# Changing how a one-core decoder-layer kernel starts: the order of its first loads, transposes and products

## Chip, core and metric

The kernel runs on one core of one Trainium2 chip. The metric is the device time in microseconds (us) of one execution; several executions of the same program are timed, and the median is compared. PE is TensorE's matmul side, PEld its weight loads, DVE VectorE, ACT ScalarE, POOL GpSimd and SP SyncE, which issues most of the DMAs here.

## What is computed

One layer of a decoder trunk, 512 tokens by 1024 features, in float32:

```python
h = x
xn = rmsnorm(h, g_attn)
proj = xn @ w_in                                   # 1024 x 3072
sb_q, sb_k, sb_v, d_q, d_k, d_v = split(proj)      # 6 x 512 columns
mix = concat(stick_breaking(sb_q, sb_k, sb_v),     # 8 heads of 64
             rmsnorm(differential(d_q, d_k, d_v, lam, rel_bias), g_subln) * 0.2)   # lambda_init 0.8, so 1 - 0.8
h = h + mix @ w_o
u = causal_depthwise_conv(rmsnorm(h, g_ffn) @ w_up, conv_w, conv_b)   # 1024 x 5632
gate, val = split(u)
h = h + (gelu(gate) * val) @ w_down
h = h + sigmoid(rmsnorm(h, g_ple) @ w_ple_gate) * (p @ w_ple_proj)
out = rmsnorm(h, g_final)
```

The stick-breaking weights are `A[t,s] = beta_ts * prod_{s<j<t}(1 - beta_tj)` with `beta = sigmoid(q k / 8)`. `lam` is `exp(lambda_q1 . lambda_k1) - exp(lambda_q2 . lambda_k2) + 0.8`, and `rel_bias` is a table that is looked up by the distance of query and key.

## The kernel before

Every float32 product is made of three matmuls (`mm3`, lines 121 to 123) on operands that are split into a rounded high part and the rest: high times high, high times low, low times high. Weights come with 1 MB or 512 KB loads on SP's queue into two buffers `wraw`; `split_w` (lines 140, 141) makes `whi` on ACT and `wlo` on DVE of 128 columns (or two row blocks) at a time, three pairs of buffers. All of x is kept transposed: eight tiles of 128 features by 512 tokens, each scaled by `g_attn` and split into `xgh` (ACT, line 330) and `xgl` (DVE, line 331).

PE runs in the order in which the code is written, by hand; the other engines' order is made by a scheduler that knows the dependences and priorities. Weight pieces stand in a list, in the order q and k of heads' pair 0, q and k of pair 1, v, and so on; `units(n)` runs the next n steps of that list, and for q, k and v one step is one feature tile, three matmuls of 512 columns. The attention's own steps (`pair_steps` for the four pairs of stick-breaking heads, `diff_steps` for the four differential heads) alternate with units by a written plan.

The start, in `stages`: x comes in four chunks of 256 features (`load_x`, line 310), 512 KB each. SP issues chunk 0, the q weights of pair 0, chunk 1, the k weights of pair 0, chunks 2 and 3, then further weights. PE runs `warm` (line 740): products of `identR` with itself, 128 columns, results unused. Then the transpose of the `g_attn` row (line 196), the eight transposes of chunk 0 (line 324), eight products more, the transposes of chunk 1, four products more, four units of piece 0 (tiles 0 to 3), the transposes of chunks 2 and 3, and the rest of pieces 0 and 1. `keep_x` copies the transposes unscaled to memory, `norm_x` makes `rstd1`, the norm of each token (POOL, line 148).

After two more units `bcast_rstd1` spreads `rstd1` over the partitions: DVE casts it (`bch`, line 154), PE runs eight small products (line 158), DVE copies the result (`rb`). Only then the q and k of pair 0, which stay in PSUM until here (`late`), can be scaled and split (lines 387 to 389). Six units later PE makes the first logits (lines 492 and 500), with two buffers `z`; ACT makes two sigmoids of each (`cum` line 524, `beta` line 525), DVE a running product (line 531). The third logits of a pair reuse the first `z`, so they wait for the second sigmoid on it.

The parameters of later stages (`params`) are loaded on ACT's queue at a place of the plan between pairs 1 and 2: gains, biases and convolution weights (lines 208 to 213), the lambdas (line 229), a table of distances (line 250). What does not depend on PE there may be put earlier by the scheduler: the two sums for `lam` on DVE (line 233) and their exp on ACT (`lexp`, line 238) run ahead of the first sigmoid.

Of the kernel before, what the change touches and what calls it, by code (L numbers as in the profile page):

```python
# [11 lines left out]
F32 = mybir.dt.float32  # L12
F32R = mybir.dt.float32r
# [5 lines left out]
P = 128  # L19
T = 512  # L20
D = 1024
KT = D // P
NB = T // P
HD = 64
# [6 lines left out]
NBUCK = 32  # L31
NMAP = 8
EPS = 1e-6
NEG = -1e30
# [4 lines left out]
YW = T + P  # L39


class Kern:
# [42 lines left out]
    def rest(self):  # L85
        for _ in self.flow:
            pass
# [36 lines left out]

    def load_w(self, src, kts, cols, raw=None):

        if raw is None:
            raw = self.wraw.tile([P, kts, cols], F32, tag="wraw", name=self.nm("wraw"))
        for off, ap in src:
            n = ap.shape[1]  # L130
            self.nc.sync.dma_start(raw[:, :, off : off + n], ap.rearrange("(k p) n -> p k n", p=P))
        return raw
# [31 lines left out]
    def consts(self):  # L164
        nc, a = self.nc, self.a
        c = self.cpool = self.open("consts")
# [31 lines left out]

    def params(self, pst):
        nc, a, c = self.nc, self.a, self.cpool  # L200

# [10 lines left out]
        self.gcol["w0"], n1 = r, r + 2 * FT  # L212
        nc.scalar.dma_start(rows2[0 : 4 * FT, :], a["conv_w"][0, 1:3].rearrange("t (r p) -> (t r) p", p=P))
        self.par = c.tile([P, n1], F32, name="par1")
        self.par2 = c.tile([P, 4 * FT], F32, name="par2")
        ps = pst()
# [6 lines left out]
        nc.vector.tensor_scalar(self.gsub, self.g("sub", 0), 1.0 - LAMBDA_INIT, None, op0=ALU.mult)  # L223


        rest = next(spare)
        lt = rest[:, : 4 * HD].rearrange("p (a d) -> p a d", a=4)
        for i, key in enumerate(("lambda_q1", "lambda_k1", "lambda_q2", "lambda_k2")):
            nc.scalar.dma_start(lt[:, i, :], a[key].partition_broadcast(P).rearrange("p o d -> p (o d)"))
        s = c.tile([P, 2], F32, name="lsum")  # L230
        junk = rest[:, 4 * HD : 5 * HD]
        for i in range(2):
            nc.vector.tensor_tensor_reduce(
                out=junk, in0=lt[:, 2 * i, :], in1=lt[:, 2 * i + 1, :], scale=1.0, scalar=0.0,
                op0=ALU.mult, op1=ALU.add, accum_out=s[:, i : i + 1],
            )
# [4 lines left out]
        nc.vector.scalar_tensor_tensor(self.neglam, e[:, 1:2], -LAMBDA_INIT, e[:, 0:1], op0=ALU.add, op1=ALU.subtract)  # L241


        tab = c.tile([NBUCK + 1, NMAP], F32, name="tab")
        nc.gpsimd.memset(tab, NEG)
        nc.scalar.dma_start(tab[0:NBUCK, :], a["rel_bias"])
        sk = self.dram.tile([NMAP, YW], F32, name="sk")
        for lo, n in ((0, T), (T, P)):
            oh, y = next(spare)[: NBUCK + 1, :n], next(spare)[:NMAP, :n]
            nc.scalar.dma_start(oh, a["onehot"][:, lo : lo + n])  # L250
# [6 lines left out]
        nc.scalar.dma_start(self.sk2, bass.AP(sk.tensor, sk.offset, [[YW, NMAP], [0, P], [1, YW]]))  # L257

# [76 lines left out]

    def behind_x(self, do):

        with self.tc.issue_after(self.last[0]), self.tc.issue_after(self.last[1]):
            do()
# [202 lines left out]
    def split_t(self, ps, n, c=""):  # L542
        nc = self.nc
        hi, lo = (x[:, :n] for x in self.parts("tw", c))
        nc.scalar.copy(hi, ps[:, :n])  # L545
        nc.vector.tensor_sub(lo, ps[:, :n], hi.bitcast(F32))  # L546
        return hi, lo
# [165 lines left out]
    def stages(self):  # L713
# [19 lines left out]
        self.xn = self.su.tile([P, NB, D], F32, name="xn")  # L733
        self.load_x((0,))
# [10 lines left out]
        def first_load():  # L745
            cols = self.qk_cols(self.qoff[0], self.koff[0])
            raw = self.load_w(cols[:1], KT, 2 * P)
            self.load_x((1,))
            self.load_w(cols[1:], KT, 2 * P, raw)
            self.load_x((2, 3))  # L750
            return raw

        self.add_qk(0)
        self.raws[0] = first_load
        self.add_qk(1)
# [7 lines left out]
        self.add_wo(4, True, lambda nt, ps: self.residual(nt, ps, "ffn", self.h1g, self.sqacc))  # L763
        self.load_raws(0)
# [5 lines left out]
        def begin(i):  # L770
            self.behind_x(lambda: self.prepare(i))
            if i < 2:
                first.append(self.pieces[i][2](*self.splits[i]))
# [12 lines left out]
        px += next(steps)  # L786
        begin(2)
        self.behind_x(self.norm_x)
        for k in range(2, KT):
            self.keep_x(k, px[k])  # L790
        todo(1, 4)
        todo(0, 5)
        todo(1, 5)
        self.flow = self._flow(2)
# [17 lines left out]

        self.units(2)
        self.bcast_rstd1(psh)
# [18 lines left out]


# [218 lines left out]
```

## Time and profile before

| | |
|---|---|
| time, median of 3 runs | 706.27 us (704.77 to 706.96) |
| the profiled execution | 706.06 us, span 704.3 us |
| PE busy | 685.5 us, 97% of the span |
| DVE, ACT, POOL busy | 441.1, 313.8, 42.5 us |
| granted TensorE clock, mean | 0.993 |

The span is the time from the first to the last instruction of the profiled execution; its own time is 1.8 us longer. A matmul's row gives a start and a modelled end; matmuls overlap, so the distance from start to start tells how fast PE goes. A 512-column product takes 0.23 us at 2.4 GHz and 0.43 to 0.44 us at 1.2 GHz. The granted clock's record begins at the first event, so its column reads 1.00 in the first 14 us too, where the starts are 0.44 us apart.

### The profile page before, as it was taken

The page shows a single profiled execution, that of the slowest core. Times are in us where ns is not written, and L with a number is a line of the kernel's source. Part 1 is how long each engine was busy: PE and PEld are TensorE (multiplying, and loading weights), DVE is VectorE, ACT ScalarE, POOL GpSimd, SP SyncE. Part 2 cuts the span into 40 slices and gives each one's busy share as a digit, 9 for nine tenths or more (in the row PEclk, how much of TensorE's full clock was granted, in tenths as well). Part 3 has the DMA queues.
Part 4 walks back from the last instruction along what each step waited for, and adds up shares of the span by engine and source line. Part 5 has one row for each costly group of instructions (what it writes and reads, how often), then busy time and mean ns, then how long its engine had stood idle before and what let it go on. Part 6 is the DMA issues. An engine that isn't in the chain of part 4 may idle for free. (4 is left out here: it accounts for less than half of the span.)

```text
span 704.3 us, 8244 instructions
## 1 busy us (share of the span) xinstructions
PE 685.5 (97%) x3263; PEld 562.3 (80%) x3263; DVE 441.1 (63%) x663; ACT 313.8 (45%) x471; POOL 42.5 (6%) x52
## 2 busy tenths in 40 slices
PE   8879999999999999999999999999999999999995
PEld 8668877787888887888888888888888888888885
DVE  3775769668666858498777777677734232436445
ACT  4654435556553543365444444444423232326422
POOL 2200000000100024100000000000000020202001
PEclk9989999999999999999999999999999999999999
DMA  9522135232326111223322233321323133127002
GB/s 288 200 69 60 60 108 192 60 94 76 106 85 209 61 60 60 90 90 121 119 77 86 78 120 119 97 84 60 123 101 105 61 104 120 45 92 239 29 27 93
DMA packets 66809, 71.64 MB, mean 102 GB/s; under 512 B 2360, under 2 KB 55850, under 8 KB 66771
## 3 DMA queue, kind: packets, MB, share of 16 engines
q1 hardware_dynamic: 63376, 64.76, 28.8%
q10 hardware_dynamic: 2755, 4.27, 1.8%
q0 software_dynamic: 640, 2.10, 0.8%
q8 instruction: 25, 0.41, 0.3%
q14 instruction: 13, 0.11, 0.0%
HBM read 66.90 MB, written 6.84 MB: 105 GB/s over the span
## 5 line engine op out<-in xcount | busy, mean ns | idle before, releaser
L140 ACT CAST whi<-wraw 128x1024 fp32r<-128x1024 f32 (+1 forms) x102 | 105.5, 1034 | 151.0 <-PE mm L122 128.3
L141 DVE TENSOR_TENSOR wlo<-wraw,whi 128x1024 fp32r<-128x1024 f32 (+1 forms) x102 | 123.5, 1211 | 74.4 <-ACT whi L140 73.4
L121 PE MATMUL mm<-xgh,whi 128*128 128x512 f32 x128 | 53.9, 421 | 0.2 <-DVE v_sb L511 0.2
L122 PE MATMUL mm<-xgl,whi 128*128 128x512 f32 x128 | 51.6, 403 | 0.0
L123 PE MATMUL mm<-xgh,wlo 128*128 128x512 f32 x128 | 51.4, 401 | 0.0
L878 DVE TENSOR_TENSOR vpad<-mm,rb 128x512 f32<-128x512 f32 x44 | 30.1, 688 | 33.8 <-PE mm L123 33.7
L699 POOL TENSOR_TENSOR sqacc<-sqacc,sq 128x512 f32<-128x512 f32 x14 | 23.1, 1653 | 359.6 <-issue 254.9
L880 ACT ACTIVATE y<-vpad,par,par 128x512 f32<-128x512 f32 x44 | 35.5, 814 | 2.7 <-DVE vpad L878 2.5
L882 DVE SCALAR_TENSOR_TENSOR y<-vpad,par,y 128x512 f32<-128x512 f32 x44 | 33.1, 751 | 1.3
L881 DVE SCALAR_TENSOR_TENSOR y<-vpad,par,y 128x512 f32<-128x512 f32 x44 | 32.8, 746 | 0.0
L121 PEld LDWEIGHTS mm<-xgh,whi 128*128 128x128 f32 x128 | 25.2, 197 | 6.8 <-issue 1.1
L884 ACT ACTIVATE y<-y 128x512 f32<-128x512 f32 x22 | 13.9, 631 | 34.9 <-DVE y L882 34.9
L123 PEld LDWEIGHTS mm<-xgh,wlo 128*128 128x128 f32 x128 | 24.9, 194 | 5.6
L122 PEld LDWEIGHTS mm<-xgl,whi 128*128 128x128 f32 x128 | 25.1, 196 | 4.6 <-DVE xgl L331 0.3
L531 DVE TENSOR_TENSOR_SCAN cum<-cum,fresh 128x512 f32<-128x512 f32 x20 | 23.6, 1212 | 4.2 <-ACT cum L524 4.2
L492 PE MATMUL z<-k,q 64*128 64x512 f32 (+3 forms) x192 | 20.6, 340 | 5.2 <-ACT beta L525 3.7
L121 PE MATMUL mm<-whi,xgh 128*128 128x512 f32 x64 | 25.5, 398 | 0.0
L122 PE MATMUL mm<-wlo,xgh 128*128 128x512 f32 x64 | 25.0, 390 | 0.0
L123 PE MATMUL mm<-whi,xgl 128*128 128x512 f32 x64 | 25.0, 390 | 0.0
L492 PEld LDWEIGHTS z<-k,q 64*128 64x128 f32 x192 | 15.5, 189 | 10.9 <-ACT beta L525 4.2
L636 ACT ACTIVATE pr<-pr,nmx 128x512 f32<-128x512 f32 (+3 forms) x32 | 17.6, 552 | 12.2 <-DVE nmx L632 12.0
L546 DVE TENSOR_TENSOR twl<-z,twh 128x1024 fp32r<-128x1024 f32 (+2 forms) x20 | 18.4, 954 | 7.1 <-ACT twh L545 7.0
(538 smaller groups left out, 1759.4 us busy)
## 6 DMA issues: line engine op xcount, KB each, us to landing
wraw<-in_w_up SPq DMA_DIRECT2D x22, 1024.0 KB, 5.0
wraw<-in_w_in SPq DMA_DIRECT2D x16, 512.0 KB, 5.2
wraw<-in_w_down SPq DMA_DIRECT2D x8, 1024.0 KB, 5.0
wraw<-in_w_in SPq DMA_DIRECT2D x4, 1024.0 KB, 6.1
wraw<-in_w_o SPq DMA_DIRECT2D x4, 1024.0 KB
wraw<-in_w_ple_gate SPq DMA_DIRECT2D x4, 1024.0 KB, 8.2
wraw<-in_w_down SPq DMA_DIRECT2D x4, 768.0 KB, 4.3
sk<-sk ACTq DMA_DIRECT2D x1, 2560.0 KB
```

The source lines that it names most:

```text
L121: nc.tensor.matmul(ps, lhsT=l[0], rhs=r[0], start=start, stop=False, **kw)
L122: nc.tensor.matmul(ps, lhsT=l[0], rhs=r[1], start=False, stop=False, **kw)
L123: nc.tensor.matmul(ps, lhsT=l[1], rhs=r[0], start=False, stop=stop, **kw)
L140: nc.scalar.copy(hi, raw)
L141: nc.vector.tensor_sub(lo, raw, hi.bitcast(F32))
L492: nc.tensor.matmul(z[:, h, col : col + n], lhsT=q[o, x, tb * P : (tb + 1) * P], rhs=k[o, y, :n], start=i == 0 and at == 0, stop=i == 2 and ...
L531: nc.vector.tensor_tensor_scan(back, back, fresh, 1.0, op0=ALU.mult, op1=ALU.max)
L699: nc.gpsimd.tensor_add(sqacc, sqacc, sq)
L878: nc.vector.tensor_mul(u[:, 2 : T + 2], ps, rb2)
L880: nc.scalar.activation(y, u[:, 2 : T + 2], AF.Identity, scale=self.cw(2, ch), bias=self.g("cb", ch))
L881: nc.vector.scalar_tensor_tensor(y, u[:, 1 : T + 1], self.cw(1, ch), y, op0=ALU.mult, op1=ALU.add)
L882: nc.vector.scalar_tensor_tensor(y, u[:, 0:T], self.cw(0, ch), y, op0=ALU.mult, op1=ALU.add)
```

## The change

The zeros: a 128x512 tile `nought` is set to zero on DVE and cast; `warm(n)` now multiplies it by itself, 512 columns a product. Nine stand first, one between the transposes of chunks 0 and 1.

The loads: the q weights of pair 0 come in two halves by rows (features 0 to 511 and 512 to 1023), the first one ahead of all x, then chunks 0 and 1, the second half, chunks 2 and 3, and only then the two halves of the k weights. Each half is cast and split by itself.

The products: after the transposes of chunk 1 two units of piece 0, the transposes of chunk 2, two units, the transposes of chunk 3, the other four units, then piece 1 (the k weights) as a whole. `split_t` now records its last instructions, and `behind_x` is called `behind`.

The broadcast: `units(5)` instead of `units(2)` stand ahead of `bcast_rstd1`; the last entry of the plan of the pairs has 8 units instead of 11.

The parameters: `params` becomes a generator. Its loads are issued from entry 4 of the plan on, the rest runs at entry 8 behind the last split. The sums and the exp for `lam` become `lambdas`, behind the last split of pair 3.

```diff
@@ consts
+        nought = su.tile([P, T], F32, name="nought")
+        nc.vector.memset(nought, 0.0)
+        self.nought = su.tile([P, T], F32R, name="noughtR")
+        nc.vector.tensor_copy(self.nought, nought)
@@ params
+        rest = next(spare)
+        lt = rest[:, : 4 * HD].rearrange("p (a d) -> p a d", a=4)
+        for i, key in enumerate(("lambda_q1", "lambda_k1", "lambda_q2", "lambda_k2")):
+            nc.scalar.dma_start(lt[:, i, :], a[key].partition_broadcast(P).rearrange("p o d -> p (o d)"))
...
+        for lo, n in ((0, T), (T, P)):
+            hot[lo] = next(spare)[: NBUCK + 1, :n]
+            nc.scalar.dma_start(hot[lo], a["onehot"][:, lo : lo + n])
+        yield
...
+    def lambdas(self):
+        nc, c = self.nc, self.cpool
+        s = c.tile([P, 2], F32, name="lsum")
+        for i in range(2):
+            nc.vector.tensor_tensor_reduce(
...
+        nc.scalar.activation(e, s, AF.Exp)
@@ stages
-                nc.tensor.matmul(busy[:, :P], lhsT=self.identR, rhs=self.identR, start=True, stop=True)
-
-        warm(12)
+                nc.tensor.matmul(busy, lhsT=self.nought[:, :P], rhs=self.nought, start=True, stop=True)
+
+        warm(9)
...
+        load(0, 0)
+        self.load_x((0, 1))
+        load(0, 1)
+        self.load_x((2, 3))
+        load(1, 0)
+        load(1, 1)
...
-        px = next(steps)
-        begin(0)
-        for k in range(2):
-            self.keep_x(k, px[k])
-        warm(8)
-        px += next(steps)
-        begin(1)
-        warm(4)
-        todo(0, 4)
+        split(0, 0)
+        px = next(steps)
+        warm(1)
+        px += next(steps)
+
+        self.behind(lambda: split(0, 1))
+        self.behind(lambda: [self.keep_x(k, px[k]) for k in range(2)])
+        todo(0, 2)
         px += next(steps)
+        todo(0, 2)
         px += next(steps)
-        begin(2)
-        self.behind_x(self.norm_x)
...
+        self.behind(lambda: [split(1, h) for h in range(2)])
         todo(0, 5)
-        todo(1, 5)
...
+        self.behind(rest)
+        todo(1, 9)
@@
-        self.units(2)
+        self.units(5)
         self.bcast_rstd1(psh)
@@
-            plan += [(p, 0, 3), (p, 1, 12), (p, 2, 4), (p, 3, 4), (p, 4, 4 if p == 2 else 11)]
+            plan += [(p, 0, 3), (p, 1, 12), (p, 2, 4), (p, 3, 4), (p, 4, 4 if p == 2 else 8)]
@@
+            if i == 4:
+                params = self.params(self.psm)
+                next(params)
             if i == 8:
-                self.params(self.psm)
+                self.behind(lambda: next(params, None))
@@
+        self.behind(self.lambdas)
```

On PE at the very start, before (`z_101` and `z_102` take the transposes of chunks 0 and 1, `mm_195` is piece 0):

```order
L740 MATMUL mm_103<-identR 128x128 x12
L196 MATMUL z_102<-ident,rows_116 128x8
L324 MATMUL z_101<-ident,xn 128x128 x8
L740 MATMUL mm_103<-identR 128x128 x8
L324 MATMUL z_102<-ident,xn 128x128 x8
L740 MATMUL mm_103<-identR 128x128 x4
L121 MATMUL mm_195<-xgh_142,whi_150 128x512
L122 MATMUL mm_195<-xgl_143,whi_150 128x512
L123 MATMUL mm_195<-xgh_142,wlo_151 128x512
```

The same place after (`mm_187` is piece 0, `mm_194` takes transposes of chunk 2):

```order
L751 MATMUL mm_106<-noughtR 128x512 x9
L200 MATMUL z_105<-ident,rows_116 128x8
L335 MATMUL z_104<-ident,xn 128x128 x8
L751 MATMUL mm_106<-noughtR 128x512
L335 MATMUL z_105<-ident,xn 128x128 x8
L121 MATMUL mm_187<-xgh_154,whi_133 128x512
L122 MATMUL mm_187<-xgl_155,whi_133 128x512
L123 MATMUL mm_187<-xgh_154,wlo_134 128x512
L121 MATMUL mm_187<-xgh_158,whi_133 128x512
L122 MATMUL mm_187<-xgl_159,whi_133 128x512
L123 MATMUL mm_187<-xgh_158,wlo_134 128x512
L335 MATMUL mm_194<-ident,xn 128x128 x4
```

The small products are gone from between the transposes, and the transposes of chunk 2 stand after two feature tiles of piece 0 instead of four.

On ACT ahead of the first sigmoid, before (`q_381` and `k_386` belong to pair 0, `mix4l` and the like are tiles that hold parameters):

```order
L388 CAST q_381<-qkt_382 128x512
L229 DMA mix4l_845<-in_lambda_q 128x64
L229 DMA mix4l_845<-in_lambda_k 128x64
L388 CAST k_386<-qkt_387 128x512
L229 DMA mix4l_845<-in_lambda_q 128x64
L229 DMA mix4l_845<-in_lambda_k 128x64
L250 DMA mix5h_846<-in_onehot 33x512
L250 DMA mix6h_848<-in_onehot 33x128
L238 ACTIVATE lexp<-lsum 128x2
L140 CAST whi_450<-wraw_247 128x1024
L388 CAST q_409<-qkt_410 128x512
L524 ACT_TABLE_LOAD
```

The same place after (the q cast of pair 0 stands just ahead; two lambdas and the one-hot tables follow behind the first two sigmoids):

```order
L140 CAST whi_410<-wraw_255 128x1024
L399 CAST k_391<-qkt_392 128x512
L213 DMA mix4h_659<-in_g_ffn 8x128
L213 DMA mix4h_659<-in_g_ple 8x128
L213 DMA mix4h_659<-in_g_subln 1x128
L399 CAST q_405<-qkt_406 128x512
L213 DMA mix4h_659<-in_conv_b 44x128
L216 DMA mix4h_659<-in_conv_w 44x128
L218 DMA mix4h_659<-in_conv_w 88x128
L222 DMA mix4l_660<-in_lambda_q 128x64
L222 DMA mix4l_660<-in_lambda_k 128x64
L535 ACT_TABLE_LOAD
```

`lexp` is gone from here, the loads of gains and convolution weights have come here from ahead of the q cast, and a weight cast stands ahead of the k cast.

On DVE ahead of the first differential head, before (`k_1402` is that head's k, `av_1355` and `v_diff` are work of pair 3 and of v):

```order
L595 TENSOR_TENSOR av_1355<-z_1356,av_1355 64x512
L832 TENSOR_TENSOR v_diff<-vd,v_diff 128x2x512 x2
L595 TENSOR_TENSOR av_1355<-z_1356,av_1355 64x512
L387 SCALAR_TENSOR_TENSOR qkt_1403<-mm_1351,rb_366 128x512
L141 TENSOR_TENSOR wlo_1408<-wraw_1279,whi_1407 128x1024
L598 TENSOR_TENSOR mix3l_1378<-av_1355,mix3h_1377 128x512
L389 TENSOR_TENSOR k_1402<-qkt_1403,k_1402 128x512
```

The same place after:

```order
L268 SCALAR_TENSOR_TENSOR neglam<-lexp 128x1
L607 TENSOR_TENSOR av_1353<-z_1354,av_1353 64x512
L862 TENSOR_TENSOR v_diff<-vd,v_diff 128x2x512 x2
L398 SCALAR_TENSOR_TENSOR qkt_1392<-mm_1340,rb_371 128x512
L607 TENSOR_TENSOR av_1353<-z_1354,av_1353 64x512
L141 TENSOR_TENSOR wlo_1397<-wraw_1268,whi_1396 128x1024
L400 TENSOR_TENSOR k_1391<-qkt_1392,k_1391 128x512
```

The last of `lambdas` stands ahead, k's scaling has moved ahead of the second `av`, and the split of pair 3's result behind k.

## Rows read from the trace of the kernel before

**Rows 1.** Windows: stretch, busy PE, PEld, DVE, ACT, POOL (count), granted clock, DMA share, GB/s

```profile
42.00:44.00 2.00, 0.55 (x4) 0.55 (x6) 1.48 (x2) 2.00 (x3) 0.00 (x0) 0.54 0.92 273
...
49.00:50.00 1.00, 1.00 (x6) 0.83 (x5) 1.00 (x2) 0.00 (x0) 0.00 (x0) 1.00 0.00 0
```

**Rows 2.** Timeline of PE's start: start, us, engine, line, operation, out<-in, count [idle before <-releaser]

```profile
1.91 2.82 PE L740 MATMUL mm<-identR 128*128 128x128 f32 x12 [1.91 <-DVE identR L181]
...
4.87 1.97 PE L324 MATMUL z<-ident,xn 128*128 128x128 f32 x8
...
8.64 1.94 PE L324 MATMUL z<-ident,xn 128*128 128x128 f32 x8 [0.20 <-DMA xn<-in_x]
...
11.12 0.73 PE L121 MATMUL mm<-xgh,whi 128*128 128x512 f32 x1
...
14.64 0.51 PE L123 MATMUL mm<-xgh,wlo 128*128 128x512 f32 x1
...
15.70 1.04 PE L324 MATMUL mm<-ident,xn 128*128 128x128 f32 x8
```

**Rows 3.** Timeline of ACT and DVE at the start, one split of a tile of x

```profile
8.38 0.69 ACT L330 ACTIVATE xgh<-z,gattn 128x512 fp32r<-128x512 f32 x1 [0.82 <-DVE xgl L331]
...
9.10 0.75 DVE L331 SCALAR_TENSOR_TENSOR xgl<-z,gattn,xgh 128x512 fp32r<-128x512 f32 x1 [0.76 <-ACT xgh L330]
```

**Rows 4.** Timeline of PE around the broadcast, the third logits, and pair 1's third logits

```profile
26.72 0.39 PE L122 MATMUL mm<-xgl,whi 128*128 128x512 f32 x1
26.95 0.39 PE L123 MATMUL mm<-xgh,wlo 128*128 128x512 f32 x1
29.45 0.33 PE L158 MATMUL z<-identR,bch 128*128 128x128 f32 x1 [2.12 <-DVE bch L154]
...
43.45 1.01 PE L492 MATMUL z<-k,q 64*128 64x256 f32 x6 [3.75 <-ACT beta L525]
...
44.87 0.73 PE L121 MATMUL mm<-xgh,whi 128*128 128x512 f32 x1
...
48.82 0.48 PE L121 MATMUL mm<-xgh,whi 128*128 128x512 f32 x1
...
69.68 0.62 PE L492 MATMUL z<-k,q 64*128 64x256 f32 x6
...
70.51 0.45 PE L121 MATMUL mm<-whi,xgh 128*128 128x512 f32 x1
```

**Rows 5.** Timelines of ACT (its queue's issues as ACTq), then of DVE, 27 to 42 us

```profile
27.02 1.04 ACT L140 CAST whi<-wraw 128x1024 fp32r<-128x1024 f32 x1
...
28.46 0.46 ACTq L211 DMA_DIRECT2D mix4h<-in_conv_w  x1
...
32.13 0.62 ACT L388 CAST q<-qkt 128x512 fp32r<-128x512 f32 x1 [4.07 <-DVE qkt L387]
...
38.49 0.20 ACT L238 ACTIVATE lexp<-lsum 128x2 f32<-128x2 f32 x1 [4.51 <-DVE lsum L233]
...
40.16 1.28 ACT L524 ACT_TABLE_LOAD   x1
41.46 1.02 ACT L524 ACTIVATE cum<-z 128x1024 f32<-128x1024 f32 x1
...
28.10 1.23 DVE L141 TENSOR_TENSOR wlo<-wraw,whi 128x1024 fp32r<-128x1024 f32 x1 [0.41 <-ACT whi L140]
29.24 0.16 DVE L154 CAST bch<-rstd 128x4 fp32r<-128x4 f32 x1
```

**Rows 6.** DMA issues: out<-in, engine, operation, count, KB each, median us to landing

```profile
wraw<-in_w_in SPq DMA_DIRECT2D x4, 1024.0 KB, 6.1
```

**Rows 7.** Waits of SP's queue: who waited for whom, us in total, times, longest

```profile
SPq L131 <- DMA mix4h<-in_conv_w: 5.3, 1, 5.3
```

**Rows 8.** Timeline of PE at the first differential head's logits

```profile
164.53 1.77 PE L492 MATMUL z<-k,q 64*128 64x512 f32 x18 [0.76 <-DVE k L389]
```

More of the change, by code (lines that the diff above doesn't have):

```diff
@@ L123, in mm3, with load_w @@
         nc.tensor.matmul(ps, lhsT=l[1], rhs=r[0], start=False, stop=stop, **kw)
-    def load_w(self, src, kts, cols, raw=None):
+    def load_w(self, src, kts, cols, raw=None, r0=0):
         if raw is None:
@@ L223, in params @@
         nc.vector.tensor_scalar(self.gsub, self.g("sub", 0), 1.0 - LAMBDA_INIT, None, op0=ALU.mult)
[L226 to L236, printed above, removed]
-        e = c.tile([P, 2], F32, name="lexp")
-        nc.scalar.activation(e, s, AF.Exp)
-        self.neglam = c.tile([P, 1], F32, name="neglam")
[L241 to L246, printed above, removed]
+        self.lt, self.junk = lt, rest[:, 4 * HD : 5 * HD]
         sk = self.dram.tile([NMAP, YW], F32, name="sk")
         for lo, n in ((0, T), (T, P)):
-            oh, y = next(spare)[: NBUCK + 1, :n], next(spare)[:NMAP, :n]
-            nc.scalar.dma_start(oh, a["onehot"][:, lo : lo + n])
+            oh, y = hot[lo], next(spare)[:NMAP, :n]
             ps = pst()
@@ L257, in params @@
         nc.scalar.dma_start(self.sk2, bass.AP(sk.tensor, sk.offset, [[YW, NMAP], [0, P], [1, YW]]))
+    def lambdas(self):
[3 more added lines that the diff above has]
+            nc.vector.tensor_tensor_reduce(
+                out=self.junk, in0=self.lt[:, 2 * i, :], in1=self.lt[:, 2 * i + 1, :], scale=1.0, scalar=0.0,
+                op0=ALU.mult, op1=ALU.add, accum_out=s[:, i : i + 1],
+            )
+        e = c.tile([P, 2], F32, name="lexp")
+        nc.scalar.activation(e, s, AF.Exp)
+        self.neglam = c.tile([P, 1], F32, name="neglam")
+        nc.vector.scalar_tensor_tensor(self.neglam, e[:, 1:2], -LAMBDA_INIT, e[:, 0:1], op0=ALU.add, op1=ALU.subtract)
     def mix_tile(self, i, x):
@@ L334, in prep_x, with behind @@
             yield banks
-    def behind_x(self, do):
+    def behind(self, do):
         with self.tc.issue_after(self.last[0]), self.tc.issue_after(self.last[1]):
@@ L544, in split_t @@
         hi, lo = (x[:, :n] for x in self.parts("tw", c))
-        nc.scalar.copy(hi, ps[:, :n])
-        nc.vector.tensor_sub(lo, ps[:, :n], hi.bitcast(F32))
+        a = nc.scalar.copy(hi, ps[:, :n])
+        b = nc.vector.tensor_sub(lo, ps[:, :n], hi.bitcast(F32))
+        self.last = (a.ins, b.ins)
         return hi, lo
@@ L739, in warm, with load @@
             for _ in range(n):
-                nc.tensor.matmul(busy[:, :P], lhsT=self.identR, rhs=self.identR, start=True, stop=True)
-        warm(12)
+                nc.tensor.matmul(busy, lhsT=self.nought[:, :P], rhs=self.nought, start=True, stop=True)
+        warm(9)
         self.params_attn(lambda: zs[1][:, 0, :])
[L745 to L751, printed above, removed]
+        half = KT // 2
+        cols = self.qk_cols(self.qoff[0], self.koff[0])
+        raw = self.wraw.tile([P, KT, 2 * P], F32, tag="wraw", name=self.nm("wraw"))
+        def load(j, h):
+            self.load_w(cols[j : j + 1], half, 2 * P, raw[:, h * half : (h + 1) * half, :], h * half * P)
+        load(0, 0)
[4 more added lines that the diff above has]
+        load(1, 1)
         self.add_qk(0)
-        self.raws[0] = first_load
+        self.raws[0], self.nraw = raw, 1
         self.add_qk(1)
@@ L768, in stages, with split, rest @@
         first = []
[L770 to L773, printed above, removed]
+        for i in range(2):
+            self.splits.append([self.wsp.tile([P, KT, P], F32R, tag=t, name=self.nm(t)) for t in ("whi", "wlo")])
+            first.append(self.pieces[i][2](*self.splits[i]))
+        def split(i, h):
+            r, k = raw[:, :, i * P : (i + 1) * P], slice(h * half, (h + 1) * half)
+            hi, lo = (x[:, k, :] for x in self.splits[i])
+            a = nc.scalar.copy(hi, r[:, k, :])
+            b = nc.vector.tensor_sub(lo, r[:, k, :], hi.bitcast(F32))
+            self.last = (a.ins, b.ins)
         todo = lambda i, n: [next(first[i], None) for _ in range(n)]
+        split(0, 0)
         px = next(steps)
-        begin(0)
-        for k in range(2):
-            self.keep_x(k, px[k])
-        warm(8)
+        warm(1)
         px += next(steps)
-        begin(1)
-        warm(4)
-        todo(0, 4)
+        self.behind(lambda: split(0, 1))
+        self.behind(lambda: [self.keep_x(k, px[k]) for k in range(2)])
+        todo(0, 2)
         px += next(steps)
+        todo(0, 2)
         px += next(steps)
-        begin(2)
-        self.behind_x(self.norm_x)
-        for k in range(2, KT):
-            self.keep_x(k, px[k])
-        todo(1, 4)
-        todo(0, 5)
-        todo(1, 5)
+        self.behind(lambda: [split(1, h) for h in range(2)])
+        todo(0, 5)
+        def rest():
+            self.prepare(2)
+            self.norm_x()
+            for k in range(2, KT):
+                self.keep_x(k, px[k])
+        self.behind(rest)
+        todo(1, 9)
         self.flow = self._flow(2)
```

9 lines of the change are left out of this document (6 added, 3 removed).

## The prediction

> **What bounds the kernel now.** First the page: PE is busy nearly the whole span, so only its waits and its clock can give time. Then the waits of PE alone: the two longest lie in the first 50 us, where the change works. There I read the timelines of PE, ACT and DVE side by side. They show four losses. The products that count start at 11.12, and the ninth starts at 14.64, so they are 0.44 us apart, against 0.23 us later (26.72 to 26.95): PE runs at 1.2 GHz, not 2.4, until then, although it had been busy with 128-column products and transposes from 1.91 on [rows 2, 4]. PE idles 2.12 us at 29.45 for the broadcast of rstd [rows 4]. It idles 3.75 us at 43.45, because ACT starts the first sigmoid only at 41.46: `lexp` had held ACT 4.51 us for the lambdas' loads, and a table load of 1.28 us came on top [rows 4, 5]. And during that idle time the granted clock falls to half (0.54 from 42 to 44, 1.00 again from 49) [rows 1].
>
> I call the 24 products of one 128-column weight piece a piece, and three products a unit. The sum is made against the profiled execution, 706.06 us (span 704.3 and 1.8 around it); the median of the runs is 706.27.
>
> **The change, part by part.**
> *Zero products.* Twelve plus twelve 128-column products become nine of 512 columns, and one more later. At 0.44 us each and from about 1.9 (the memset and cast of zeros on DVE take the place of the wait for `identR`, [rows 2]) nine end at 5.9. Before, PE reached the first transposes at 4.87, so this alone costs about 1 us. It pays only if the clock is full afterwards. The trace of before does not show a product on zeros, so the value lies between no effect and full clock from about 6. I take full clock: both times that PE ran 512-column products without a break from half clock, it had it after eight or nine of them, 11.12 to 14.64 and 44.87 to 48.82 [rows 2, 4].
>
> *Loads.* The last x chunk has 2.5 MB ahead of and with it, not 3; the second 1.25, not 1.5. PE waited for the second until 8.64 [rows 2]; five sixths of that is 7.2, I take 7.5. The last was there by 15.70 with 3 MB, so by 13.1 with 2.5. The halved weights cost one issue more on SP and land early; ACT has cast the first half before x is there, so nothing on the path.
>
> *Alternation.* With the clock full: transposes of chunk 0 (1.04 us for eight [rows 2]) 5.9 to 6.9, of chunk 1 7.5 to 8.5. ACT and DVE then split four tiles in turn at 0.69 and 0.75 [rows 3]: 8.0 + 2 x 0.69 + about 0.8 puts the second tile's low half at 10.2. Six products end at 10.65, chunk 2 at 11.65, six more (6 x 0.227) at 13.0, chunk 3 at 14.0. Then 42 products are left of the 54 that stand ahead of the broadcast before: 14.0 + 9.55 + 0.25 for the last tile's split = 23.8, where before had 15.70, sixteen transposes and the same 42 and was done at 27.2.
>
> *Broadcast nine products later* (units 5, not 2, ahead of it). PE gets there at 23.8 + 9 x 0.227 = 25.85. DVE's order still puts a weight split ahead of the broadcast's cast, as before (28.10, then 29.24 [rows 5]). That split needs a 1 MB load into the buffer of the first weights, free when DVE has split their last half: chunk 3's tiles until 16.45, two half splits 17.7. Load 6.1 [rows 6], cast 1.04, split 1.23, then 0.4: the broadcast is at **26.5**, a wait of 0.65. If that load landed earlier, the wait is nothing; if it took 2 us more, 2.65. Gain here: 29.45 - 26.5, plus nine products already done, 2.05: **5.0**.
>
> *Parameters' work later.* `lexp`, the two reductions and their wait leave ACT and DVE. From the broadcast, the q cast comes 2.68 later (32.13 [rows 5]) and lasts 0.62; then the order has a weight cast (1.04) and the k cast (0.62): 5.0 after the broadcast. Then eight issues of parameters' loads on ACT, which before stood mostly ahead of the broadcast: 0.3 to 0.46 each (one is 0.46 [rows 5]), 3 to 3.5, the third q cast runs beside them; the table load 1.28, two sigmoids of 1.02 less 0.1 overlap, and 0.3 for the steps between: 11.9 after the broadcast the first z is free. PE has the broadcast, 18 products and two logits to do, of which the logits wait for k's low half (behind the k cast on DVE, at about 6.4); I put its arrival at 11.1, so it waits 0.8. Before, that distance was 43.45 - 29.45 = 14.0 with the same 18 products. Gain: **2.15**. The bounds: no wait at all gives 2.95; eight issues that each wait for a landing give nothing.
>
> *The clock.* Without 3.75 us of idling it should not fall. Before, the third logits took 44.87 - 43.45 = 1.42 against 70.51 - 69.68 = 0.83, and nine products 48.82 - 44.87 = 3.95 against 2.05 [rows 4]. Gain: **2.5**; nothing if it falls all the same.
>
> *Where the three units are given back.* Ahead of the first differential head, 8 units stand where 11 stood. Before, PE waited 0.76 there for k's low half on DVE [rows 8]. PE now arrives up to 2.05 earlier on a DVE chain (two value splits, a copy, a weight split, k) that is as long; `lambdas` adds small work in front of it, hidden behind the last transposes' split. Some of DVE's chain was idle, so I take a loss of **1.0**, between 0 and 2.05. The exp table load moves with `lexp` and replaces that of the head: nothing.
>
> Sum: 5.0 + 2.15 + 2.5 - 1.0 = 8.65, so 706.06 - 8.65 = **697.4**.
>
> **The rivals.**
> *The clock is not carried by this start.* For: before, 9 us of transposes and 128-column products, 1.91 to 11.12, left the clock at half [rows 2], and now transposes stand between products three times, and nothing shows what zeros do. Against: the sixteen transposes from 15.70 did not cost the clock once it was full, and nine products are what it took at 44.87. The Trainium skill, "TensorE: Matmul & The Clock Gate", Part 4, says that the full clock does not engage for transposes, which do not count as PE being busy in the same way; the trace agrees for the raising and shows nothing of the kind for the falling. At half clock: chunk 0 until 7.6, one zero product, chunk 1 9.7, six products 12.3, chunk 2 14.0, six 16.6, chunk 3 18.3; if eight more products are done at half clock, as from 11.12, that is 21.8, and 34 + 9 at 0.227 give 31.6 for the broadcast. The first term becomes 29.45 - 31.6 + 2.05 = -0.1, the total 3.55: **702.5**. A clock that is raised and falls once lies between, about 699.5.
>
> *The wait for the sigmoid stays*, since eight issues on ACT take the lambdas' place. If the distance from broadcast to the third logits stays at 14.0 and the clock falls, 2.15 and 2.5 are gone: **702.0**. Together with the first rival it is 707, no change.
>
> *All three waits that I put in* (0.65, 0.8 and 1.0) *are not there*: **695.0**.
>
> *Slower*: ACT now issues four loads, two lambdas and the one-hot tables, between the first and the second pair of sigmoids, and these issues wait on semaphores shared in turn with SP's loads; before, SP once waited 5.3 us for a parameter to land [rows 7]. Everything behind on ACT waits: the second sigmoids, DVE's scans, then PE's transposes of pair 0, 45 products after the third logits. By my chain DVE is done 2.4 us ahead of PE there; each us beyond goes to PE, and the clock falls once more (2.5). It decides from 2.4 + 8.65 - 2.5 = 8.6 us of waiting; at 11 us it gives about **708.5**. Against: the weights it would wait for are issued as soon as DVE has split a piece, some 6 us ahead.
>
> **How the numbers follow.** About 0.3%, 2.1 us, is what a measurement of this kernel can tell from no change: 704.15 and 708.4 are the bounds. Forecast (696 to 699.5, a clock that falls once included) 0.56; clock not carried 0.20; sigmoid's wait stays 0.11; none of my three waits 0.07; both first rivals together 0.04; slower 0.02. The range from 694.5 to 703 leaves out the last two and some of the edges. Faster 0.94 - 0.01 for unknowns = 0.93, same 0.04, slower 0.03.
>
> **What would show it.** Right: products 0.23 apart by 10 us, the broadcast's first product near 26.5 after 63 products, the first sigmoid about 10 after it, third logits near 38.4 with a wait under 1.5, granted clock 1.00 from 40 to 50, and the wait ahead of the first head near 1.8. Wrong: products 0.44 apart after 12 us; an ACT queue row with a long wait between the sigmoids; a PE wait of over 2 us at the broadcast. Most of all the forecast hangs on the clock in the first 20 us.

## The result

| | before | after |
|---|---|---|
| time, median of ten runs each | 706.02 us (704.61 to 707.97) | 700.94 us (699.61 to 704.40) |
| ratio after to before, 95% interval | | 0.9933 (0.9916 to 0.9951) |
| the profiled execution, and its span | 706.06, 704.3 | 700.64, 698.8 |
| granted TensorE clock, mean | 0.993 | 0.996 |

Faster by 5.1 us. The forecast was 697.4, 8.65 us less than before, so the sign and the range (694.5 to 703) held and the size did not; the time lies outside the forecast's own band of 696 to 699.5. The rows of after answer to those of before in the order of the stages; the first group is PE's start (start, us, engine, line, operation, out<-in, count, idle time before and its releaser), against [rows 2].

```profile
1.93 4.21 PE L751 MATMUL mm<-noughtR 128*128 128x512 f32 x9 [1.93 <-DVE noughtR L177]
...
6.26 1.65 PE L335 MATMUL z<-ident,xn 128*128 128x128 f32 x8
...
8.37 1.06 PE L335 MATMUL z<-ident,xn 128*128 128x128 f32 x8 [0.22 <-DMA xn<-in_x]
...
10.79 0.50 PE L121 MATMUL mm<-xgh,whi 128*128 128x512 f32 x1 [0.58 <-ACT xgh L341]
11.66 0.50 PE L122 MATMUL mm<-xgl,whi 128*128 128x512 f32 x1 [0.37 <-DVE xgl L342]
...
12.22 1.04 PE L335 MATMUL mm<-ident,xn 128*128 128x128 f32 x8
```

The clock is full from the second half of chunk 0's transposes on (1.65 us for eight, then 1.06), as forecast. But chunk 1 comes at 8.37, not 7.5, and the second feature tile holds PE twice. ACT in the same stretch, against [rows 3]:

```profile
7.95 0.69 ACT L341 ACTIVATE xgh<-z,gattn 128x512 fp32r<-128x512 f32 x1 [3.55 <-PE z L335]
9.47 1.26 ACT L341 ACTIVATE xgh<-z,gattn 128x512 fp32r<-128x512 f32 x2 [0.83 <-PE z L335]
10.98 0.69 ACT L341 ACTIVATE xgh<-z,gattn 128x512 fp32r<-128x512 f32 x1 [0.24 <-DVE xgl L342]
...
13.02 1.29 ACT L341 ACTIVATE xgh<-mm,gattn 128x512 fp32r<-128x512 f32 x2
```

ACT begins when all eight transposes of chunk 0 are done (6.26 + 1.65 = 7.91), although four of them make a whole feature tile. The row at 9.47 holds two tiles. The first is one of chunk 1, since it waited for that chunk's transposes; chunk 0's second tile comes only behind it, done at 10.73, and PE's product of it waits until 10.79. The last tile, which shares the two-bank PSUM tile `z` with the one at 9.47, waits 0.24 for DVE to be done with that one; the tiles of chunk 2, each in an `mm` of its own, go back to back at 13.02. PE further on, against [rows 4] and [rows 8]; the first logits of before are the row behind it:

```profile
28.02 0.22 PE L158 MATMUL z<-identR,bch 128*128 128x128 f32 x1
...
34.53 0.96 PE L503 MATMUL z<-k,q 64*128 64x512 f32 x6 [1.34 <-DVE k L400]
...
39.33 0.62 PE L503 MATMUL z<-k,q 64*128 64x256 f32 x6
...
47.08 0.50 PE L121 MATMUL mm<-whi,xgh 128*128 128x512 f32 x1 [1.25 <-DVE qkt L398]
...
72.21 0.50 PE L121 MATMUL mm<-xgh,whi 128*128 128x512 f32 x1 [1.17 <-DVE v_sb L522]
...
158.81 1.78 PE L503 MATMUL z<-k,q 64*128 64x512 f32 x18 [1.79 <-DVE k L400]
```

```profile
34.84 0.96 PE L492 MATMUL z<-k,q 64*128 64x512 f32 x6
```

The waits of 2.12 at the broadcast and of 3.75 at the third logits are gone. New are 1.34 at the first logits, 1.25 at 47 and 1.17 at 72 (0.22 at that place before), and the wait at the first differential head has grown from 0.76 to 1.79. The sigmoids on ACT come without `lexp`, against [rows 5]:

```profile
34.87 1.28 ACT L535 ACT_TABLE_LOAD   x1 [1.56 <-DMA mix4h<-in_conv_w]
...
36.16 1.03 ACT L535 ACTIVATE cum<-z 128x1024 f32<-128x1024 f32 x1
...
37.08 1.02 ACT L536 ACTIVATE beta<-z 128x1024 f32<-128x1024 f32 x1
```

And the windows of 42 to 44 and 48 to 50 (busy PE, PEld, DVE, ACT, POOL with counts, granted clock, DMA share, GB/s) keep the full clock where [rows 1] had 0.54:

```profile
42.00:44.00 2.00, 2.00 (x10) 1.65 (x9) 1.97 (x2) 2.00 (x4) 0.00 (x0) 1.00 0.16 51
...
48.00:50.00 2.00, 2.00 (x11) 1.64 (x10) 1.53 (x3) 1.06 (x1) 0.00 (x0) 1.00 0.03 8
```

### The profile page after: what moved, and what is told of

Same layout as the page of the kernel before. It is cut to its first block, busy times and chain, and to the rows that moved or that the text cites. A ratio compares the mean times of both kernels' runs of the same rounds, so it can differ in the third digit from the quotient of the medians.

```text
span 698.8 us, 8222 instructions
## 1 busy us (share of the span) xinstructions
PE 680.0 (97%) x3249; PEld 555.7 (80%) x3249; DVE 441.8 (63%) x667; ACT 314.4 (45%) x473; POOL 42.7 (6%) x52
## 5 line engine op out<-in xcount | busy, mean ns | idle before, releaser
L140 ACT CAST whi<-wraw 128x1024 fp32r<-128x1024 f32 (+1 forms) x100 | 103.4, 1034 | 143.4 <-PE mm L122 116.6
L141 DVE TENSOR_TENSOR wlo<-wraw,whi 128x1024 fp32r<-128x1024 f32 (+1 forms) x100 | 121.0, 1210 | 70.7 <-ACT whi L140 69.6
```

Source lines behind the costliest of these rows:

```text
L140: nc.scalar.copy(hi, raw)
L141: nc.vector.tensor_sub(lo, raw, hi.bitcast(F32))
```

## The experiments

Theory: the change is three things, each with its own worth: the parameters' work, the start, and the three units put ahead of the broadcast. The rivals are named with each run. Differences are of medians, each kernel against the runs of before on its own chip (706.0 to 706.6).

| kernel | median, us | less than before | ratio, 95% interval |
|---|---|---|---|
| after | 700.94 | 5.1 | 0.9916 to 0.9951 |
| params_only | 701.52 | 4.6 | 0.9925 to 0.9956 |
| start_only | 704.34 | 1.8 | 0.9967 to 0.9995 |
| noshift | 699.38 | 7.2 | 0.9878 to 0.9915 |
| plan_b | 700.25 | 5.8 | 0.9906 to 0.9934 |
| plan_a | 699.05 | 7.0 | 0.9885 to 0.9914 |
| small_warm | 701.11 | 5.5 | 0.9906 to 0.9942 |
| no_warm | 701.43 | 5.2 | 0.9910 to 0.9956 |
| noalt | 700.81 | 5.5 | 0.9912 to 0.9950 |
| ones | 700.57 (one run) | 6.0 | none |
| banks | 698.78 | 7.5 | 0.9881 to 0.9911 |
| banks_small | 698.09 | 8.2 | 0.9878 to 0.9908 |
| plan_a_banks | 696.84 | 9.4 | 0.9855 to 0.9884 |

### The two halves alone

*params_only* is the kernel before with `params` as a generator and `lambdas` behind pair 3:

```diff
+            if i == 4:
+                params = self.params(self.psm)
+                next(params)
             if i == 8:
-                self.params(self.psm)
+                self.behind(lambda: next(params, None))
...
+        self.behind(self.lambdas)
```

> The kernel before with the parameters' part of the change alone (loads at entry 4, the rest at entry 8 behind a split, the lambdas' sums and exp behind pair 3); start, loads and plan as before. My theory: the parameters' gain does not need the new start. The broadcast stays near 29.45 us, the third logits come near 41.0 (distance about 11.5, before 14.0), the granted clock does not fall from 40 to 50: 2.5 + 2.5 us, about 701.0. If the two waits that are new in the changed kernel (1.25 us for pair 1's scaling near 47, 1.0 for the first v split near 72) come from the parameters' move, they are seen here too and the time is about 703.2; if they come from the three units put ahead of the broadcast, they are not. Rival: the sigmoid's chain follows the first weights' landing and not the parameters; then the pause at the third logits stays above 3 us and the time is 706.

Most of the gain is here. PE reaches the third logits 11.65 us after the broadcast, without a wait; of the new waits only 0.37 at pair 1's scaling is seen, and 0.22 and 0.76 stand at the two later places as before.

```profile
29.34 0.33 PE L158 MATMUL z<-identR,bch 128*128 128x128 f32 x1 [2.07 <-DVE bch L154]
...
40.99 0.62 PE L499 MATMUL z<-k,q 64*128 64x256 f32 x6
...
49.90 0.50 PE L121 MATMUL mm<-whi,xgh 128*128 128x512 f32 x1 [0.37 <-DVE qkt L394]
...
160.15 1.77 PE L499 MATMUL z<-k,q 64*128 64x512 f32 x18 [0.76 <-DVE k L396]
```

Here the 2.07 us wait at the broadcast was followed by half the clock, which the 2.12 us of before was not (windows as above):

```profile
30.00:32.00 2.00, 2.00 (x8) 1.81 (x8) 0.92 (x2) 0.00 (x0) 0.00 (x0) 0.50 1.01 383
32.00:34.00 2.00, 2.00 (x7) 1.58 (x7) 1.75 (x3) 0.82 (x2) 0.00 (x0) 0.68 0.13 45
```

*start_only* is the changed kernel with the parameters as they were:

```diff
-            if i == 4:
-                params = self.params(self.psm)
-                next(params)
             if i == 8:
-                self.behind(lambda: next(params, None))
+                self.params(self.psm)
...
-        self.behind(self.lambdas)
```

> The changed kernel with the parameters' work as it was before (loads at entry 8 in one go, lambdas' sums and exp ahead of the first sigmoids); start, loads, alternation and the three units as changed. My theory: the start's gain is its own, 3.5 us at the broadcast (28.0 against 29.45, with nine products more done), 1.0 is lost at the first differential head, and the pause at the third logits and the fall of the clock stay: 706.0 - 3.5 + 1.0 = 703.5, and about 704.8 if the 1.25 us wait for pair 1's scaling belongs to this part. Rival: the lambdas land at a fixed time after the start, so PE's lead at the broadcast turns into a longer pause there (over 6 us): about 707. Together with the run of the parameters alone: if both gains are independent, the two differences from before add up to that of the changed kernel, 5.1 us.

The time fits the theory (between its two values, 703.5 and 704.8), but the pause is not where it put it: there is none at the third logits. The scheduler now puts the lambdas' sums and `lexp` between the sigmoids, with two table loads more; DVE's scans end later, and PE waits 3.45 us at pair 1's scaling. Behind that wait the clock was at half (0.50 from 50 to 54) in this execution, which took 706.48, 2.1 more than the median. ACT, then DVE, then PE there:

```profile
42.98 1.28 ACT L242 ACT_TABLE_LOAD   x1
44.54 0.20 ACT L242 ACTIVATE lexp<-lsum 128x2 f32<-128x2 f32 x1 [0.27 <-DVE lsum L237]
44.76 1.28 ACT L528 ACT_TABLE_LOAD   x1
```

```profile
44.27 0.23 DVE L237 CUSTOM_DVE_ANT_0 mix4l<-mix4l 128x64 f32<-128x64 f32 x1 [1.37 <-DMA mix4l<-in_lambda_k]
```

```profile
49.79 0.79 PE L121 MATMUL mm<-whi,xgh 128*128 128x512 f32 x1 [3.45 <-DVE qkt L391]
```

4.6 and 1.8 together are 6.4, more than the 5.1 of both. With intervals of about 1 us to either side this only hints that the halves share part of their gain.

### The three units ahead of the broadcast

*noshift* takes them back:

```diff
-        self.units(5)
+        self.units(2)
...
-            plan += [(p, 0, 3), (p, 1, 12), (p, 2, 4), (p, 3, 4), (p, 4, 4 if p == 2 else 8)]
+            plan += [(p, 0, 3), (p, 1, 12), (p, 2, 4), (p, 3, 4), (p, 4, 4 if p == 2 else 11)]
```

> The changed kernel with two units ahead of the broadcast and eleven at the plan's last entry, as before, everything else as changed. Theory: PE is at the broadcast 2.05 us earlier and waits there for the cast of rstd, which comes at 27.4: broadcast near 27.6 with a wait of some 1.5; in return the three waits that the changed kernel has and the one before had not (qkt at 47, 1.25; v_sb at 72, 1.2 against 0.2; first differential head 1.8 against 0.8) are as before, so the three units were worth 0.5 or less: 700.0 to 701.0. Rival (the units' 2.05 us are kept): 702.5 or more.

The time is below the theory's span: without this part the change is worth 7.2 us, not 5.1. A wait of 1.33 comes back at the broadcast, and the three others shrink:

```profile
27.27 0.33 PE L158 MATMUL z<-identR,bch 128*128 128x128 f32 x1 [1.33 <-DVE bch L154]
...
47.80 0.50 PE L121 MATMUL mm<-whi,xgh 128*128 128x512 f32 x1 [0.36 <-DVE qkt L398]
...
71.97 0.50 PE L121 MATMUL mm<-xgh,whi 128*128 128x512 f32 x1 [0.22 <-DVE v_sb L522]
...
158.07 1.78 PE L503 MATMUL z<-k,q 64*128 64x512 f32 x18 [0.76 <-DVE k L400]
```

0.89 + 0.95 + 1.03 = 2.9 is given back there, and 1.34 at the first logits, against 1.33 gained at the broadcast. All four waits are for DVE. At the last three PE has three units less to do ahead of DVE's result. At the first logits DVE itself is later: k's low half is done 4.6 us after the broadcast in noshift and 6.4 in after, where a scaling of pair 1 and a weight split stand ahead of it. Two smaller waits go the other way (0.40 and 0.65 in noshift, 0.43 in after), so 2.3 is left. (In this execution, too, the clock was 0.59 and 0.55 from 28 to 32, so its span of 698.1, 0.7 below that of after, could have been some 1.7 shorter.)

*plan_b* and *plan_a* keep the units ahead of the broadcast and move others within the plan:

```diff
-        plan = [(0, 0, 3), (0, 1, 15), (0, 2, 4), (0, 3, 4), (1, 0, 3), (1, 1, 15), (0, 4, 4), (1, 2, 4), (1, 3, 4), (1, 4, 4)]
+        plan = [(0, 0, 5), (0, 1, 13), (0, 2, 4), (0, 3, 4), (1, 0, 3), (1, 1, 15), (0, 4, 4), (1, 2, 4), (1, 3, 4), (1, 4, 4)]
```

That is plan_b; plan_a has `(0, 0, 5), (0, 1, 10)` there, and 11 at the plan's last entry.

> The changed kernel with 5 and 13 units behind the first two steps of pair 0 (3 and 15 changed), nothing else. My theory: only the wait for pair 1's scaling at 47 goes (1.25 us), the two others stay: 699.7. Rival (DVE bound there): it moves, 700.9.

> The changed kernel with another split of the plan: 5 and 10 units behind the first two steps of pair 0 (3 and 15 changed), 11 units at the last entry (8 changed), so that pair 1's k is complete two units after the first sigmoids and the first differential head has its eleven units again. My theory: the three waits that the changed kernel has and the kernel before had not (1.25 us for pair 1's scaling at 47, 1.0 at the first v split at 72, 1.0 more at the first differential head at 159) come from where units stand, not from DVE's load; all three shrink to under 0.4 each and the time is about 698. Rival: DVE is the bound in these stretches, and PE meets the same delay at its next need of DVE; then the waits move and the time stays at 700.9 within 0.7.

plan_b: the wait at 47 is gone, 1.17 and 1.79 stay, 0.7 less than after: theory, though the intervals overlap. plan_a: the waits at 47 and 72 are gone or 0.2, the one at the head is back to 0.76, with 0.73 new at pair 0's transposes; 1.9 less than after, where the theory had about 2.9. Waits of plan_a's PE (who waited for whom, us in total, times, longest):

```profile
PE z L503 <- DVE k L400: 2.1, 2, 1.3
...
PE z L588 <- DVE beta L543: 1.1, 2, 0.7
...
PE mm L121 <- DVE v_sb L522: 0.2, 1, 0.2
```

So DVE is not the bound there. Where the units stand decides.

### The clock at the start, and the alternation

*small_warm* puts twice as many 128-column products, which take the same time, in place of the zeros:

```diff
-                nc.tensor.matmul(busy, lhsT=self.nought[:, :P], rhs=self.nought, start=True, stop=True)
+                for _ in range(2):
+                    nc.tensor.matmul(busy[:, :P], lhsT=self.identR, rhs=self.identR, start=True, stop=True)
```

*no_warm* has `warm(1)` for `warm(9)` and none between the chunks; *ones* has `memset(nought, 1.0)`; *noalt* takes the alternation back:

```diff
-        todo(0, 2)
+        todo(0, 4)
         px += next(steps)
-        todo(0, 2)
         px += next(steps)
```

> The changed kernel with its zero products (9 and 1 of 512 columns) replaced by twice as many of 128 columns on the identity, which take the same time (0.23 us each where the others take 0.44), as the kernel before had them. Theory (512-column products are what raises the clock): PE reaches the transposes as early as before, but the first products are 0.43 apart until some eight are done, the transposes take 1.95 for eight; the broadcast comes 2 to 3.5 us later, 30.0 to 31.5, and the time is 703 to 704.5. Rival (any activity of PE of this length raises it): as the changed kernel, 700.9, products 0.23 apart from 9.5 us on.

> The changed kernel with one zero product in place of ten, ahead of everything else; PE then idles until the first chunk of x is there. Theory: the clock is half until some eight 512-column products are done, as with the small products, so the same 703 to 704.5; the transposes of chunk 0 may start earlier than 6.26, which gains nothing, because chunk 1 lands at 8.4 to 9.1 anyhow. Rival: x and the splits alone set the start, and the clock of the first 15 us is hidden behind them: 700.9.

> The changed kernel with ones in place of zeros in the products whose results are not used. Both theories that tell the clock by the products' columns expect the same as the changed kernel: full clock by the first product that counts, 700.9 within the spread of its runs (699.6 to 704.4). If the zeros mattered, the start's products would be 0.23 or 0.43 apart where the changed kernel's are not.

> The changed kernel with four feature tiles' products together behind chunk 1 and chunks 2 and 3 transposed together behind them, as the kernel before had it; loads and zero products as changed. Theory: PE must wait for the splits of tiles 2 and 3 ahead of chunk 2's transposes, so these come at about 14 and the splits of chunks 2 and 3 follow later; the 54th product starts 0.8 to 1.5 us later than in the changed kernel (25.8), and the broadcast about 29. Rival: the alternation is worth nothing and the loads' order all; then the 54th product starts at 25.8 within the scatter that the landing of x brings (0.4).

Here my theory fell. With small products PE is at half clock until 12.4, for four products where I expected some eight, and it costs nothing:

```profile
8.98 1.94 PE L335 MATMUL z<-ident,xn 128*128 128x128 f32 x8 [0.29 <-DMA xn<-in_x]
...
12.43 0.40 PE L122 MATMUL mm<-xgl,whi 128*128 128x512 f32 x1
...
12.89 1.03 PE L335 MATMUL mm<-ident,xn 128*128 128x128 f32 x8
```

From chunk 1's transposes to chunk 2's it takes 12.89 - 8.98 = 3.91 us, at half clock but for the last two products, and without a wait for a split. It takes 12.22 - 8.37 = 3.85 in the changed kernel at full clock, which there has waits of 0.58 and 0.37 instead. Five other executions at full clock with the same alternation (start_only, plan_a, plan_b, noshift, ones) give 3.83 to 3.86. At full clock ACT and DVE set this distance, and on ACT it is the order that is seen above: chunk 0's second tile stands behind a tile of chunk 1. ACT in plan_b, whose chunk 0 was transposed 0.7 earlier, shows it: it idles 1.87 us for chunk 1's transposes, while DVE was done with chunk 0's first tile at 8.67.

```profile
9.76 1.27 ACT L341 ACTIVATE xgh<-z,gattn 128x512 fp32r<-128x512 f32 x2 [1.87 <-PE z L335]
```

Without the zeros, chunk 2 even came at 11.69:

```profile
5.89 3.68 PE L335 MATMUL z<-ident,xn 128*128 128x128 f32 x16 [2.96 <-DMA xn<-in_x]
9.21 0.78 PE L121 MATMUL mm<-xgh,whi 128*128 128x512 f32 x1
...
11.69 1.04 PE L335 MATMUL mm<-ident,xn 128*128 128x128 f32 x8
```

noalt: the rival was right. Chunk 2 is transposed at 13.41, but chunk 3 at 14.29 (14.48 after), and the 54th product starts at 25.57 (25.76 after). ones behaves like zeros: eight transposes of chunk 0 in 1.09 us, full clock. So neither the zeros nor the alternation is by itself worth anything that can be measured. Whether one of them must be there, or the loads' order does it all, no run tells: both were never taken away together, and the loads' order was never changed alone.

### Own PSUM tiles

*banks* gives each of the six tiles of chunks 0, 1 and 3 a PSUM tile of its own until the start is over; *banks_small* adds the small products.

```diff
+        psS = self.open("psS", bufs=1, space=PSUM)
+        one = lambda i: psS.tile([P, T], F32, tag=f"s{i}", name=self.nm("s"), bufs=1)
...
-        banks = [zs[0][:, 0, :], zs[0][:, 1, :], zs[1][:, 0, :], zs[1][:, 1, :]]
-        banks = itertools.chain(banks, (f() for f in (self.psm, self.psm, psh, psh)))
+        banks = (f() for f in (*(lambda i=i: one(i) for i in range(4)), self.psm, self.psm, lambda: one(0), lambda: one(1)))
```

> The changed kernel with each transposed feature tile of chunks 0, 1 and 3 in a PSUM tile of its own, where two shared one. Theory: in the changed kernel ACT and DVE take turns on a shared tile and ACT waits for all eight transposes of a chunk, and this, not the clock, sets the 3.85 us from the transposes of chunk 1 to those of chunk 2; with own tiles the distance falls to the work of PE at full clock (0.82 + 6 x 0.23 and a little, 2.4 to 2.8), the waits of 0.6 and 0.4 at the second feature tile and 0.3 at the last one go, and the broadcast comes about 1 us earlier for the same landing of x. The time falls by less, 700 to 700.9, since PE then meets the later waits (scaling of pair 1, first v split) earlier. Rival: the landing of chunk 2 holds PE; then a wait for x stands at chunk 2 and nothing is gained.

> The same own tiles, and the small 128-column products of equal time in place of the zero products. Theory: with the shared tiles gone the clock counts: half at the first products, so chunk 2's transposes follow chunk 1's by 1.6 + 6 x 0.43, about 4.0 less what the clock gives back when it rises, 3.5 to 4.0, against 2.4 to 2.8 with the zero products. Rival (the clock costs nothing in the first 13 us whatever stands there): the same distance in both.

The distance falls to 11.08 - 8.69 = 2.39, and the time by 2.2 against after, more than I expected. ACT starts its two tiles of chunk 0 at 7.35, after four transposes, and goes without turns (PE's rows, those of banks_small behind them, then banks' ACT):

```profile
8.69 1.09 PE L335 MATMUL s<-ident,xn 128*128 128x128 f32 x8 [0.71 <-DMA xn<-in_x]
...
11.08 1.09 PE L335 MATMUL mm<-ident,xn 128*128 128x128 f32 x8
```

```profile
8.76 1.97 PE L335 MATMUL s<-ident,xn 128*128 128x128 f32 x8
...
12.19 1.04 PE L335 MATMUL mm<-ident,xn 128*128 128x128 f32 x8
```

```profile
7.35 1.27 ACT L341 ACTIVATE xgh<-s,gattn 128x512 fp32r<-128x512 f32 x2 [3.05 <-PE s L335]
9.38 1.27 ACT L341 ACTIVATE xgh<-s,gattn 128x512 fp32r<-128x512 f32 x2 [0.77 <-PE s L335]
```

With that, chunk 0's second tile also stands ahead of chunk 1 on ACT. So banks changes the order as well as the sharing, and no run tells what each is worth. The broadcast comes at 26.46, 1.56 earlier than in after, and the later waits do not grow (1.33, 1.04, 1.17 and 1.79), against the theory; so the gain is kept.

The Trainium skill, "PSUM — Partial Sum Buffer" ("PSUM bank collisions raise a hardware error"), has software keep two engines apart within a bank and quadrant. The two halves of `z` are 512 float32 columns each, a bank apiece by that page, so by its rule the turns between them are not the chip's demand. The runs agree: with a tile for each, ACT takes the two of a chunk back to back.

With the small products the distance is 12.19 - 8.76 = 3.43, so the clock now buys 1.0 us at chunk 2, about as the theory has it. At the broadcast 0.46 is left (26.46 against 26.92, with PE waiting 0.44 in the faster one), and the times, 698.78 and 698.09, do not tell them apart.

### Both together

*plan_a_banks* has own tiles and plan_a's plan.

> Own PSUM tiles and the plan with 5 and 10 units behind pair 0's first steps and 11 at the end. Theory: with no later wait that grows when PE comes earlier, the start's gain of about 1 us is kept: 698.0 to 698.6. Rival: the chain from broadcast over sigmoids and scans on ACT and DVE holds pair 0's transposes at the same distance from the broadcast's cast, which does not move: 699.1 as without the own tiles.

696.84 us, the fastest kernel here: 9.4 us less than before, 4.1 less than after, whose interval its own does not touch. The start's gain is kept, and more than the 1 us of the theory. Three of PE's waits from the broadcast on:

```profile
26.26 0.33 PE L158 MATMUL z<-identR,bch 128*128 128x128 f32 x1 [0.68 <-ACT xc L355]
...
32.88 0.96 PE L503 MATMUL z<-k,q 64*128 64x512 f32 x6 [1.36 <-DVE k L400]
...
155.22 1.77 PE L503 MATMUL z<-k,q 64*128 64x512 f32 x18 [0.75 <-DVE k L400]
```

## Why the prediction was right, and where its size was wrong

- *Parameters and the clock in the forties* (2.15 + 2.5 = 4.65). Right: params_only measures 4.6. That it agrees to 0.1 is luck, since its profiled execution lost clock from 30 to 34 within the same stretch. The third logits come 39.33 - 28.02 = 11.3 us after the broadcast (forecast 11.9, before 14.0), with no wait where 0.8 was put. The wait for k at the first logits (1.34), 6.5 us after the broadcast, was in the sum: the forecast had 6.4. The issues on ACT, on which the second rival and the slower one rested, held its table load for 1.56 us, and PE at the third logits not at all. The 2.5 rests on one trace of before; one run of that kernel on record has a mean clock of 0.996 and took 706.10 all the same, so it is not shown that each of its runs has that fall.
- *The start, as far as PE's arrival at the broadcast* (25.85). The step that failed: PE was there at 28.02, after 27.80 for the last of the products. Three terms were too small. Chunk 1's transposes began at 8.37, not 7.5 (+0.9). With the same loads chunk 1 was there by 7.65 in no_warm and only at 9.07 in plan_a, so a landing scaled by the megabytes ahead was no sure term. From chunk 1 to chunk 2 I had 10.65 - 7.5 = 3.15 and it took 3.85 (+0.7). The turns were in the sum, but I let ACT begin after four of chunk 1's transposes, and it began after eight, 1.1 us behind their start in place of 0.5. And from the start of chunk 3's transposes to the end of the 54th product I had 10.8 and it took 11.5 (+0.7): the splits held PE, last at 18.59, for longer than the 0.25 I had put.
- *Full clock from 6 us on*, on which the forecast "most of all" hung: it came, and was worth nothing that can be measured, since ACT and DVE set the pace. So the right sign does not come from it. For the same reason the first rival (702.5 at half clock) was mis-priced: small_warm is that case, at 701.1.
- *The broadcast's cast* behind a weight split: forecast 26.1, in the trace about 27.4, and covered by PE's later arrival; the wait of 0.65 did not come.
- *Nine products earlier* (2.05, less 1.0 given back at the head). The loss at the head was 1.03, as put. But the same units had also covered DVE at pair 1's scaling (1.25, of which 0.36 stays without them) and at the first v split (1.17, of which 0.22 stays). Neither is in the sum. The wait for k at the first logits (1.34), which is in it, comes from these units too: without them it is gone. I looked only at the place from which the units were taken in the plan, not at each place where PE now comes earlier than DVE. By noshift the term is not +1.05 but 5.1 - 7.2, about -2, with some 1 us to either side.

By spans the sum closes: (29.45 - 28.02) + 2.05 at the broadcast, 14.0 - 11.31 behind it, 2.5 of clock, less 1.25, 0.95 and 1.03 at the three waits, is 5.4; the spans differ by 704.3 - 698.8 = 5.5. (Smaller waits between pairs, 0.6 less in after, and small losses elsewhere about cancel.) So of the 8.65, 1.5 is missing at the broadcast (3.5 for 5.0), 0.5 more was won behind it, and 2.2 went into the two waits that were not in the sum.

## What to carry to other kernels

When work is moved ahead on the bottleneck engine, walk the whole plan behind it and ask at each hand-over whether the other engine's chain comes earlier too; what was cover in one place is a wait in three others. Before buying clock for a start, ask who paces it: at half and at full clock PE took the same 3.9 us here, and the zeros were worth nothing that could be measured, while buffers of their own for the transposed tiles, with the order on ACT that came with them, were worth 2.2 us.

## What the runs showed of the hardware

*A short wait is sometimes followed by half the clock.* The wait of 1.79 at the first differential head stands in nine profiled executions; the clock fell behind it in one, plan_b's:

```profile
158.38 2.40 PE L503 MATMUL z<-k,q 64*128 64x512 f32 x18 [1.79 <-DVE k L400]
```

```profile
158.00:160.00 2.00, 1.62 (x13) 1.60 (x15) 1.46 (x5) 0.00 (x0) 0.00 (x0) 0.82 0.01 4
160.00:162.00 2.00, 2.00 (x11) 1.69 (x9) 1.87 (x11) 1.88 (x5) 0.00 (x0) 0.50 0.00 0
162.00:164.00 2.00, 2.00 (x9) 1.31 (x8) 1.41 (x8) 1.61 (x8) 0.00 (x0) 0.82 0.00 0
```

(0.18 + 0.50 + 0.18) x 2 = 1.7 us are lost. The wait of some 1.3 at the first logits stands in eleven and was followed by half the clock in one (banks_small); of the broadcast's waits 2.12 was not, 2.07 and 1.33 were. So a wait of that length costs its own time and now and then up to 1.7 more; less where the next wait shrinks by it (in banks_small the 1.04 that banks has at pair 1's scaling is gone). It may show in the scatter: plan_a, whose longest wait behind the start is 1.34, ran from 698.74 to 699.62, after from 699.61 to 704.40. That each of after's longer runs had such a fall was not seen; their mean clock (0.992 to 0.994 in the four longest, 0.998 in the shortest) speaks for it. In the runs of before the two do not go together (706.48 at 0.995, 705.20 at 0.992).

*What stood ahead of the clock's rise at the start.* Behind nine 512-column products on zeros or ones it was full at some time between about 6 and 8 us. Behind eighteen 128-column products of the same length it was at half; it rose only when one (banks_small) or four (small_warm) products of 512 columns had followed, and in the kernel before, behind twenty-four small ones, when eight had. The Trainium skill, "TensorE: Matmul & The Clock Gate", Part 1, says that the number of products at half clock differs from run to run of one kernel. No run here shows that, since each kernel has one trace; between kernels it differs as said.
